# A transformer block on one core: all eight gate pairs by seven block products, a second buffer for the convolution's input, early results stored from ScalarE, the last merged block split by halves

## The chip, the cores and the metric

The kernel runs on one core of a Trainium2 chip, in one launch. The metric is the device time in microseconds (us), and a kernel's time is the median of its runs. Five engines work in parallel, each through its own instructions in a fixed order: TensorE (PE: matmuls, with its weight loads listed as PEld), VectorE (DVE), ScalarE (ACT), GpSimd (POOL) and SyncE (SP). Here SyncE starts most loads, and GpSimd most stores. An engine that waits for another one holds back everything that stands behind the waiting instruction in its own order.

## The reference

One layer of a decoder block on 1024 positions of width 1024. The token mixer takes one modulated, normalised input `h`:

```python
def hybrid_mixer(h, w_in, conv_w, conv_b, conv_ln_g, conv_ln_b, w_conv_out, w_att_out, w_o):
    proj = h @ w_in
    glu_in, qkv, gates = jnp.split(proj, [2 * CONV_WIDTH, 2 * CONV_WIDTH + 3 * ATT_WIDTH], axis=-1)
    u_val, u_gate = jnp.split(glu_in, 2, axis=-1)
    u = u_val * jax.nn.sigmoid(u_gate)
    u = causal_depthwise_conv(u, conv_w, conv_b)
    u = jax.nn.silu(layernorm(u, conv_ln_g, conv_ln_b))
    y_conv = u @ w_conv_out
    qkv = qkv.reshape(b, s, 3, N_HEADS, HEAD_DIM)
    o = stick_breaking_attention(qkv[:, :, 0], qkv[:, :, 1], qkv[:, :, 2])
    y_att = o.reshape(b, s, ATT_WIDTH) @ w_att_out
    g_conv, g_att = jnp.split(gates, 2, axis=-1)
    merged = jax.nn.sigmoid(g_conv) * y_conv + jax.nn.sigmoid(g_att) * y_att
    return merged @ w_o
```

`CONV_WIDTH` and `ATT_WIDTH` are 512, so `gates` is a product of 1024x1024 by 1024x2048. Around the mixer stand norms, a residual, and a feed-forward sub-layer (SwiGLU), which the change doesn't touch.

## The kernel before

Activations lie with channels on the 128 partitions and positions along the free side: `h` is eight tiles of 128x1024, each held as a high part `hhi` and a low part `hlo` (the rest after the high part's rounding). Every product of two matrices is made of three: high by high, high by low and low by high. A weight is loaded raw, ScalarE copies its high part and VectorE subtracts to get the low part (`load_w`, L151 to L159, and `w_op`, L388 to L392). Loads go through SyncE's queue (`load`, L97) and stores through GpSimd's (`store`, L100).

The order of each engine's instructions is not the order of the code. A framework places tiles in pools with a given number of buffers per tag, simulates the program once, and fixes an order for each engine. An edit in one place can therefore move instructions elsewhere.

The mixer's stages around the change, in time:

1. The convolution (`conv`, L438 to L460) of four blocks of channels, as matmuls of 128x128 (L453) of weights `cvw` on a padded copy `ph` of the block. `ph` has one buffer (tag "ph"): it is loaded (L441) from `v_d` in memory, when the block before it has been read to its end. The fourth, `conv(3)`, runs beside attention.
2. Attention, head by head: scores `z` (L543 and L544), transposes `tr` (L566), outputs `av` (L575 and L576). PE works at other products while ScalarE and VectorE work at the scores.
3. The gates. The sixteen blocks of 128 gate channels form eight pairs. A plain pair (the loop over `PLAIN`, L604 to L612) is two products of the whole `h`, two results `pg` of 128x512 per block: 48 matmuls of 128x512 per block, 96 per pair. The other way treats a pair's weights and `h` as 2x2 blocks and makes the four result blocks from seven block products of 12 matmuls each, 84 per pair, with sums of blocks (Winograd's form of Strassen's scheme). With `NPL = 1`, pairs 0 to 6 (`GPAIRS`) take the seven products, and pair 7 is plain.
4. Of the seven, two need only plain blocks of `h`, so they are made early: `early(i, q)` (L615 to L625) loads the raw weight `ew` (q = 0), splits it into `a` (L147 and L391), makes the product `k` (`prod0`, L404, 12 matmuls), evacuates it on ScalarE to `ee` (L624, two buffers of tag "sg"), and stores it through GpSimd (L625): the first product to `e_d0[i]`, the sum of both, after a sigmoid, to `s_d[2 * i]`. Weights `ew` share the three buffers of tag "wraw" with the other raw weights.
5. The other five (`other_five`, L697 to L721) need sums of blocks of `h`, the forms T1 to T4 (L664 to L682). For each j of 0 to 3 four tiles `f` are loaded from `xm_d`, combined on VectorE (L674 to L677), and split into a high part (ScalarE, L147) and a low part (VectorE, L660): `T1o` to `T4o`. The first product of a pair is T2 by `s2o` into the bank `ka`. The weights `gw` of the pair and the early result `ga` are loaded by `pair_load` (L687); VectorE forms the weight sums `gs` (L702 to L707) and the result sums `gv` and `gw` (L710 to L720).
6. The convolution's layer norm (`ln_all`, L737 to L787) with loads `cr` from `u_d`, sums on VectorE (L747, L749, L755) and four small matmuls (L751, L761); then `y_conv` (L795 to L810).
7. Attention's output projection `pya` with the merge (L828 to L844). For each block n of 128 channels the merged `yc` is split into `mhi[n]` and `mlo[n]` as a whole 128x1024 tile (`split_r`, L728: the copy on ScalarE is L147, the subtraction on VectorE L728).
8. The output projection `pwo` (L900) reads `mhi` and `mlo`.

Of the kernel before, what the change touches and what calls it, by code (L numbers as in the profile page):

```python
# [10 lines left out]
F32 = mybir.dt.float32  # L11
F32R = mybir.dt.float32r
AF = mybir.ActivationFunctionType
ALU = mybir.AluOpType
# [3 lines left out]
P = 128  # L18
D = 1024
T = 1024  # L20
KT = D // P
CH = 512
# [6 lines left out]
NG = P // CG  # L29
TM = T // PH  # L30
SH = (TAPS - 2) // PH + 2
# [4 lines left out]
SH_DVE = (5, 6, 7)  # L36
NADA = 5
LATER = 100000
NPL = 1
GORDER = (0, 1, 2, 3, 4, 5, 6, 7)  # L40
NXT = 6
NWT = 4
# [27 lines left out]
def tile_block(ctx: ExitStack, tc: tile.TileContext, xT, vecs, ada1, ada2, win, wv, wcv, wat, wo, w1, w2, cvw, out):  # L70
    nc = tc.nc
    act, dve, pool, pe = nc.scalar, nc.vector, nc.gpsimd, nc.tensor

    def mkpool(stack, name, bufs=1, **kw):
        return stack.enter_context(tc.tile_pool(name=name, bufs=bufs, reuse_waits="tile", **kw))
# [3 lines left out]
    hp = mkpool(ctx, "hp", 16)  # L79
# [6 lines left out]
    s_d = [dp.tile([P, T], F32, name=f"s_d{n}") for n in range(2 * KT)]  # L86
    e_d0 = [dp.tile([P, CH], F32, name=f"e_d0_{i}") for i in range(KT)]
# [9 lines left out]
    def load(dst, src):  # L97
        return nc.sync.dma_start(dst, src)

    def store(dst, src):  # L100
        nc.gpsimd.dma_start(dst, src)
# [43 lines left out]
    def copy_to(eng, dst, src):  # L145
        if eng is act:
            act.activation(dst, src, AF.Copy)  # L147
        else:
            eng.tensor_copy(dst, src)
# [41 lines left out]
    def bank(name):  # L191
        return psm.tile([P, CH], F32, tag="main", name=name)
# [188 lines left out]
    mhi, mlo = [], []  # L381
    HK = KT // 2
    GP = dve
    GPAIRS = GORDER[:KT - NPL]
    PLAIN = [2 * i + q for i in GORDER[KT - NPL:] for q in range(2)]
    B0 = {}

    def w_op(name, src, hi_eng, lo_eng):  # L388
        t = wp.tile([P, 2, CH], F32R, tag=("whi", "wlo")[next(uid) % 2], name=name)
        copy_to(hi_eng, t[:, 0], src)  # L390
        lo_eng.tensor_tensor(t[:, 1], src, t[:, 0], op=ALU.subtract)  # L391
        return t[:, 0], t[:, 1]  # L392

    def prod0(bank_, w, b, first=True):
        for j in range(HK):
            cols = slice(j * P, (j + 1) * P)
            if b[0] == "T":
                mvs = B0[b, j][:, 0], B0[b, j][:, 1]
            else:
                k = j + (HK if b in ("B21", "B22") else 0)  # L400
                cs = slice(CH, T) if b == "B22" else slice(0, CH)
                mvs = hhi[k][:, cs], hlo[k][:, cs]
            for s, (st, mv) in enumerate(((0, 0), (0, 1), (1, 0))):
                pe.matmul(bank_, w[st][:, cols], mvs[mv], start=(first and j == 0 and s == 0),  # L404
                          stop=(j == HK - 1 and s == 2), skip_group_check=not first)

    with ExitStack() as sC:
        pc = mkpool(sC, "pc")
        with ExitStack() as sA:
# [26 lines left out]
                load(channels(v_d[ct]), u)  # L436

            def conv(ct):  # L438
                ph = pc.tile([P, NG, SH - 1 + TM], F32, tag="ph", name=f"ph{ct}", bufs=1)
                pool.memset(ph[:, :, 0:SH - 1], 0.0)  # L440
                load(ph[:, :, SH - 1:], v_d[ct].rearrange("g p m -> p g m"))  # L441
                wts = []
                for hf in range(2):
                    cv = bank(f"pcv{ct}_{hf}")
                    o = sgp.tile([P, NG // 2, TM], F32, tag="sg", name=f"co{ct}_{hf}", bufs=2)
                    for gi in range(NG // 2):
                        g = hf * (NG // 2) + gi
                        for d in range(SH):
                            n, at = divmod((g * SH + d) * P, T)
                            if n == len(wts):  # L450
                                wts.append(wp.tile([P, T], F32, tag="wraw", name=f"cvw{ct}_{n}"))
                                load(wts[n], cvw[ct, n])
                            pe.matmul(cv[:, gi * TM:(gi + 1) * TM], wts[n][:, at:at + P],  # L453
                                      ph[:, g, SH - 1 - d:SH - 1 - d + TM], start=(d == 0), stop=(d == SH - 1))
                    for gi in range(NG // 2):
                        b = C_CB + ct * NG + hf * (NG // 2) + gi
                        act.activation(o[:, gi], cv[:, gi * TM:(gi + 1) * TM], AF.Identity, bias=vec[:, b:b + 1],
                                       scale=1.0)
                    load(u_d[ct][hf * (NG // 2):(hf + 1) * (NG // 2)].rearrange("g p m -> p g m"), o)
# [155 lines left out]
            def early(i, q):  # L615
                if q == 0:
                    raw = wp.tile([P, T], F32, tag="wraw", name=f"ew{i}")
                    load(raw, win[20 + 2 * i])
                    kes[i] = bank(f"k_{i}"), raw
                k, raw = kes[i]  # L620
                w = w_op(f"a1{q + 1}_{i}", raw[:, q * CH:(q + 1) * CH], act, dve)
                prod0(k, w, ("B11", "B21")[q], q == 0)
                e = sgp.tile([P, CH], F32, tag="sg", name=f"ee{q}_{i}", bufs=2)
                act.activation(e, k, (AF.Copy, AF.Sigmoid)[q])  # L624
                store(s_d[2 * i][:, :CH] if q else e_d0[i], e)  # L625

            for n, i in enumerate(GPAIRS):
                early(i, 0)
# [5 lines left out]
    with ExitStack() as sG:  # L634
# [19 lines left out]
        def flat(t):  # L654
            return t.rearrange("p a b -> p (a b)")
# [9 lines left out]
        for j in range(HK):  # L665
            if j == 0:
                f = [pg.tile([P, T], F32, tag="f", name=f"f{q}_{j}", bufs=2) for q in range(2)]
# [57 lines left out]
        def split_r(src, names, hi_eng, lo_eng):  # L725
            hi, lo = (hp.tile([P, T], F32R, tag="act", name=nm) for nm in names)
            copy_to(hi_eng, hi, src)
            lo_eng.tensor_tensor(lo, src, hi, op=ALU.subtract)  # L728
            return hi, lo
# [91 lines left out]
        for p in range(4):  # L821
            of = wp.tile([P, T], F32, tag="wraw", name=f"of{p}")
            load(of, o_d[p])
            hi, lo = (flat(ot(f"{nm}{p}", F32R)) for nm in ("ohi", "olo"))
# [5 lines left out]
        for n in range(KT):  # L830
            if n % 2 == 0:
                wa = load_w(wat[n // 2], f"wa{n}", act, dve)
            sg = [xt(f"sga{n}_{c}") for c in range(NCH)]
            yb = {c: bkg(f"pya{n}_{c}") for c in range(NCH)}
            gemm(yb, wa, (ohi, olo), range(4), woff=(n % 2) * CH)
            y = yc[n]
            for c in range(NCH):
                cs = slice(c * CH, (c + 1) * CH)
                load(sg[c], s_d[8 + n][:, cs])
                last = dve.tensor_tensor(sg[c], yb[c], sg[c], op=ALU.mult)  # L840
                dve.tensor_tensor(y[:, cs], y[:, cs], sg[c], op=ALU.add)
            hi, lo = split_r(y, (f"mhi{n}", f"mlo{n}"), act, dve)
            mhi.append(hi)
            mlo.append(lo)  # L844
        assert not a2
        add_bias(16, 32)
        fold_gate(gpost1, 16, C_POST1)
# [641 lines left out]
    with ExitStack() as sG:  # L1489
# [233 lines left out]
        for m in range(2):  # L1723
            load(ytile["c11", m], c11_d[:, 2 * m:2 * m + 2])
            for i in range(2):
                y = ytile["c11", m][:, i]
                act.activation(y, y, AF.Copy, scale=gpost2[:, 2 * m + i:2 * m + i + 1])
        c21 = out_tiles("c21", (h_tile, h_tile))
        for h in range(2):
# [7 lines left out]
            for n in range(NH):  # L1737
                sq = sq_tile(f"fsq{h}_{n}")[:, :W]
                y = ka[n][:, cols]
                if h == 0:  # L1740
                    y = c21[n][:, cols]
# [74 lines left out]
```

## Time and profile before

The profile is one execution; its own time is a little above the median of the timed runs.

| what | value |
|---|---|
| median of 3 runs | 1413.03 us |
| lowest and highest of them | 1412.89 and 1413.87 us |
| the profiled execution's own time | 1414.92 us |
| its span, first to last instruction | 1413.2 us |
| mean granted clock of PE | 0.99 of full speed |
| busy, share of the span | PE 98%, DVE 74%, ACT 46%, POOL 8% |

Times in the rows of the trace count from the start of the span. A row of the timeline gives start, length (both in us), engine, line, operation, result and operands, how many in a run, and in square brackets the idle time before it with what ended it. A row of the list of waits gives who waited for whom, with the total, the number of times and the longest. "PEclk" in a window is the clock granted to PE, 1.00 for full speed.

### The profile page before, as it was taken

To read this page: it belongs to the slowest core of one execution; us is meant where nothing else is said; L and a number is where in the kernel's file an instruction comes from. 1 tells how busy PE (TensorE), PEld (TensorE's weight loads), DVE (VectorE), ACT (ScalarE), POOL (GpSimd) and SP (SyncE) were. 2 spreads that over 40 slices of the span, in tenths; PEclk is the share of its full clock that TensorE was granted. 3 is DMA by queue.
4 is the path that set the end of the run, shared out by engine and by line. 5 is a ranking of instruction groups with operands and counts; after the bars stand their busy time and mean duration, and the time that the engine had idled before them with its cause. 6 is when DMAs were issued, how large, how long until landed. Compare 5 with 4: busy or idle time off the path is not lost.

```text
span 1413.2 us, 18854 instructions
## 1 busy us (share of the span) xinstructions
PE 1378.3 (98%) x6810; PEld 1157.3 (82%) x6810; DVE 1048.3 (74%) x1591; ACT 655.3 (46%) x1146; POOL 117.4 (8%) x262
## 2 busy tenths in 40 slices
PE   7999999999998999999999999999999999999996
PEld 5898898998886788788877778888888887888886
DVE  7897687675865888878589878778877776785355
ACT  6375566364554455512356553334434443434441
POOL 0100001000001111000011110001111110000002
PEclk8999999999999999999999999999999999999998
DMA  9512051140348554973934545456777769586736
GB/s 382 200 39 82 16 164 30 46 150 30 120 150 298 208 170 148 349 226 124 360 120 163 182 148 177 165 171 212 260 250 246 264 240 387 177 337 221 254 116 120
DMA packets 93789, 265.02 MB, mean 188 GB/s; under 512 B 10048, under 2 KB 21440, under 8 KB 92672
## 3 DMA queue, kind: packets, MB, share of 16 engines
q1 hardware_dynamic: 74352, 201.68, 42.0%
q0 software_dynamic: 19344, 62.14, 12.4%
q8 instruction: 53, 0.87, 0.3%
q14 instruction: 40, 0.33, 0.1%
HBM read 192.74 MB, written 71.04 MB: 187 GB/s over the span
## 4 chain that ended last, share of the span: by engine, by line
PE 75%; issue 9%; DVE 8%; DMA 4%; ACT 2%; POOL 1%; SPq 0%; DVEq 0%; POOLq 0%; ACTq 0%
PE ka L982 14%; PE ka L1524 9%; PE kc L982 8%; PE pwo L900 6%; PE pb L1524 4%; PE pgv L168 3%; PE pv L473 3%; PE pgg L168 2%; PE pk L168 2%; PE pq L168 2%; PE ke L1090 2%; PE pcv L453 2%; PE tr L566 2%; PE pa L1524 2%; PE kb L982 2%
## 5 line engine op out<-in xcount | busy, mean ns | idle before, releaser
L545 ACT ACTIVATE ka<-z 128x128 f32<-128x128 f32 (+2 forms) x96 | 47.0, 496 | 55.8 <-PE z L544 51.9
L551 DVE TENSOR_TENSOR_SCAN ka<-ka,eye 128x128 f32<-128x128 f32 (+1 forms) x64 | 52.1, 831 | 23.2 <-ACT ka L545 23.0
L570 DVE TENSOR_TENSOR alo<-tr,ahi 128x512 fp32r<-128x512 f32 x80 | 53.4, 685 | 21.3 <-ACT ahi L569 20.7
L569 ACT ACTIVATE ahi<-tr 128x512 fp32r<-128x512 f32 x80 | 46.7, 603 | 39.1 <-PE av L575 22.9
L1524 PE MATMUL ka<-gt,w2f 128*128 128x512 f32 x264 | 63.4, 389 | 0.0
L556 DVE TENSOR_TENSOR be<-be,ka 128x127 f32<-128x127 f32 (+2 forms) x96 | 51.2, 550 | 12.1 <-ACT be L547 8.5
L1524 PEld LDWEIGHTS ka<-gt,w2f 128*128 128x128 f32 x264 | 49.5, 188 | 10.3
L123 DVE SCALAR_TENSOR_TENSOR ada<-ada,cb 128x1024 f32<-128x1024 f32 x32 | 38.9, 1223 | 23.6 <-DMA ada<-in_ada_dram 23.4
L1090 PE MATMUL ke<-b,w_hi 128*128 128x512 f32 x176 | 55.2, 395 | 0.0
L547 ACT ACTIVATE be<-z 128x127 f32<-128x127 f32 (+2 forms) x96 | 46.4, 496 | 17.8 <-PE tr L566 17.6
L566 PE MATMUL tr<-ident,be 128*128 128x128 f32 x288 | 46.6, 272 | 0.0
L453 PE MATMUL pcv<-ph,cvw 128*128 128x128 f32 x320 | 43.7, 282 | 2.5 <-DMA ph<-v_d 2.5
L554 DVE TENSOR_TENSOR_SCAN ka<-ka 128x512 f32<-128x512 f32 x32 | 40.4, 1274 | 6.3 <-ACT ka L545 6.3
L404 PE MATMUL k<-hhi,a 128*128 128x512 f32 x112 | 38.3, 413 | 6.6 <-ACT ee L624 6.6
L453 PEld LDWEIGHTS pcv<-ph,cvw 128*128 128x128 f32 x320 | 41.5, 198 | 3.5 <-issue 2.7
L575 PE MATMUL av<-ahi,vst 128*128 128x256 f32 x160 | 43.8, 291 | 0.0
L576 PE MATMUL av<-alo,vst 128*128 128x256 f32 x160 | 42.2, 290 | 0.0
L1090 PEld LDWEIGHTS ke<-b,w_hi 128*128 128x128 f32 x176 | 32.9, 188 | 7.9 <-issue 1.0
L147 ACT ACTIVATE gt<-X 128x512 fp32r<-128x512 f32 x33 | 20.3, 629 | 39.4 <-DVE X L1567 14.3
L473 PE MATMUL pv<-wv_hi,hhi 128*128 128x256 f32 x128 | 36.7, 287 | 1.6 <-DVE vst L478 0.9
L147 ACT ACTIVATE s1o<-s 128x512 fp32r<-128x512 f32 x22 | 13.8, 629 | 48.8 <-PE ka L982 41.0
L473 PE MATMUL pv<-wv_lo,hhi 128*128 128x256 f32 x128 | 36.3, 285 | 0.0
(545 smaller groups left out, 4145.8 us busy)
## 6 DMA issues: line engine op xcount, KB each, us to landing
w_d<-w2o POOLq DMA_DIRECT2D x44, 512.0 KB, 7.6
w2f<-w_d SPq DMA_DIRECT2D x44, 512.0 KB, 4.5
ada<-in_ada_dram SPq DMA_DIRECT2D x32, 512.0 KB, 5.7
w2r<-in_w_dram SPq DMA_DIRECT2D x44, 256.0 KB, 3.8
w1g<-in_w_dram SPq DMA_DIRECT2D x21, 512.0 KB, 3.7
w1u<-in_w_dram SPq DMA_DIRECT2D x21, 512.0 KB, 5.7
cvw<-in_cvw_dram SPq DMA_DIRECT2D x20, 512.0 KB, 3.8
ada_w<-in_ada_dram SPq DMA_DIRECT2D x8, 1024.0 KB, 13.9
```

The costliest lines, as they stand in the source:

```text
L168: pe.matmul(bank, st[:, cols], mv[k][:, c * CH:(c + 1) * CH], start=(i == 0 and s == 0), stop=(i == n - 1 and s == 2))
L453: pe.matmul(cv[:, gi * TM:(gi + 1) * TM], wts[n][:, at:at + P], ph[:, g, SH - 1 - d:SH - 1 - d + TM], start=(d == 0), stop=(d == SH - 1))
L473: pe.matmul(pv[:, :256], st[k][:, tcols], mv[:, wc], start=(k == 0 and i == 0), stop=(k == KT - 1 and i == 2))
L545: act.activation(kap[:, s_lo:s_hi], z[:, zo:zo + w], AF.Sigmoid, bias=0.0, scale=-0.125)
L551: dve.tensor_tensor_scan(rev, rev, eye[:, CH - w:][:, ::-1], 0.0, op0=ALU.mult, op1=ALU.add)
L556: dve.tensor_tensor(beta[:, :m], beta[:, :m], kap[:, s_lo + 1:s_lo + 1 + m], op=ALU.mult)
L566: pe.transpose(tr[:, o:o + P], src, ident)
L570: dve.tensor_tensor(alo, tr, ahi, op=ALU.subtract)
L900: pe.matmul(bank_, st[:, cols], mv[k][:, cs], start=(k == 0 and q == 0), stop=(k == KT - 1 and q == 2))
L982: pe.matmul(bank_, st[:, cols], t[:, mv], start=(first and j == 0 and s == 0), stop=(j == HK - 1 and s == 2), skip_group_check=not first)
L1090: pe.matmul(kbs[f], wes[f][st][:, cols], t[:, mv], start=(i == 0 and j == 0 and q == 0), stop=(j == HK - 1 and q == 2), skip_group_check=i ...
L1524: pe.matmul(dst, w[st][:, cols], g[mv], start=first and s == 0, stop=last and s == 2, skip_group_check=more)
```

## The change

Four edits:

- `NPL` goes from 1 to 0: pair 7, too, is made by seven products; `PLAIN` is empty.
- `ph` has two buffers instead of one.
- The sixteen early results are started by ScalarE instead of GpSimd.
- The last merged block (n = 7) is split into its parts by halves of 512 columns, each right after its sum; the other seven are split whole, as before.

```diff
--- before.py
+++ after.py
@@ -36,7 +36,7 @@
 SH_DVE = (5, 6, 7)
 NADA = 5
 LATER = 100000
-NPL = 1
+NPL = 0
 GORDER = (0, 1, 2, 3, 4, 5, 6, 7)
 NXT = 6
 NWT = 4
@@ -436,7 +436,7 @@
                 load(channels(v_d[ct]), u)
 
             def conv(ct):
-                ph = pc.tile([P, NG, SH - 1 + TM], F32, tag="ph", name=f"ph{ct}", bufs=1)
+                ph = pc.tile([P, NG, SH - 1 + TM], F32, tag="ph", name=f"ph{ct}", bufs=2)
                 pool.memset(ph[:, :, 0:SH - 1], 0.0)
                 load(ph[:, :, SH - 1:], v_d[ct].rearrange("g p m -> p g m"))
                 wts = []
@@ -622,7 +622,7 @@
                 prod0(k, w, ("B11", "B21")[q], q == 0)
                 e = sgp.tile([P, CH], F32, tag="sg", name=f"ee{q}_{i}", bufs=2)
                 act.activation(e, k, (AF.Copy, AF.Sigmoid)[q])
-                store(s_d[2 * i][:, :CH] if q else e_d0[i], e)
+                act.dma_start(s_d[2 * i][:, :CH] if q else e_d0[i], e)
 
             for n, i in enumerate(GPAIRS):
                 early(i, 0)
@@ -839,9 +839,17 @@
                 load(sg[c], s_d[8 + n][:, cs])
                 last = dve.tensor_tensor(sg[c], yb[c], sg[c], op=ALU.mult)
                 dve.tensor_tensor(y[:, cs], y[:, cs], sg[c], op=ALU.add)
-            hi, lo = split_r(y, (f"mhi{n}", f"mlo{n}"), act, dve)
-            mhi.append(hi)
-            mlo.append(lo)
+                if n < KT - 1:
+                    continue
+                if c == 0:
+                    mhi.append(hp.tile([P, T], F32R, tag="act", name=f"mhi{n}"))
+                    mlo.append(hp.tile([P, T], F32R, tag="act", name=f"mlo{n}"))
+                act.activation(mhi[n][:, cs], y[:, cs], AF.Copy)
+                dve.tensor_tensor(mlo[n][:, cs], y[:, cs], mhi[n][:, cs], op=ALU.subtract)
+            if n < KT - 1:
+                hi, lo = split_r(y, (f"mhi{n}", f"mlo{n}"), act, dve)
+                mhi.append(hi)
+                mlo.append(lo)
         assert not a2
         add_bias(16, 32)
         fold_gate(gpost1, 16, C_POST1)
```

The order of every engine's instructions changes from `conv(3)` on, and is the same again from the output projection on. Three places follow.

On PE, around the start of `conv(3)` (`tr`, `z` and `av` belong to attention; `pcv_0_4111` is the first half of `conv(3)`), as one piece of the difference, after (+) against before (-):

```order
 L566 MATMUL tr_0_0_0_3844<-ident,zeros 128x128
 L566 MATMUL tr_0_0_0_3844<-ident,be_0_1_0_3835 128x128
+L453 MATMUL pcv_0_4111<-ph_4108,cvw_0_4113 128x128
 L543 MATMUL z_1_6_0_3907<-kst_1_3035,qst_1_3033 128x512
 L544 MATMUL z_1_6_0_3907<-klo_1_3037,qst_1_3033 128x512
+L453 MATMUL pcv_0_4111<-ph_4108,cvw_0_4113 128x128
 L543 MATMUL z_1_7_0_3915<-kst_1_3035,qst_1_3033 128x512
 L544 MATMUL z_1_7_0_3915<-klo_1_3037,qst_1_3033 128x512
...
 L543 MATMUL z_1_4_1_3950<-kst_1_3035,qst_1_3033 128x256
 L544 MATMUL z_1_4_1_3950<-klo_1_3037,qst_1_3033 128x256
-L453 MATMUL pcv_0_4111<-ph_4108,cvw_0_4113 128x128 x8
```

Two of the first eight matmuls are seen to move up, and six more (four and two) stand in the rows left out; all eight are now among attention's products ahead of `z_1_4_1`, where before they came behind it.

On SyncE, at the end of attention, before (`o_d` is attention's output, `f` the tiles of the forms, `ada` weights of a later stage, `ew` an early weight, `gw0a` and `gw0b` the weights of pair 0):

```order
L98 DMA o_d_69<-oT_3610 128x1024
L98 DMA ew_4476<-in_win_dram 128x1024
L98 DMA f_0_4585<-xm_d_103 128x512 x2
...
L98 DMA f_3_4656<-xm_d_106 128x512
L98 DMA ew_4515<-in_win_dram 128x1024
L98 DMA gw0a<-in_win_dram 128x1024
L98 DMA ada_16_5535<-in_ada_dram 128x1024
L98 DMA ada_17_5538<-in_ada_dram 128x1024
L98 DMA gw0b<-in_win_dram 128x1024
L98 DMA f_3_4657<-xm_d_110 128x512
L98 DMA f_3_4658<-xm_d_110 128x512
```

And now (`cr` are the layer norm's loads):

```order
L98 DMA gw0b<-in_win_dram 128x1024
L98 DMA o_d_69<-oT_3610 128x1024
L98 DMA gw1a<-in_win_dram 128x1024
L98 DMA f_0_4500<-xm_d_103 128x512 x2
...
L98 DMA f_3_4571<-xm_d_106 128x512
L98 DMA cr_4909<-u_d_74 128x1024
...
L98 DMA cr_4912<-u_d_77 128x1024
L98 DMA ada_16_5553<-in_ada_dram 128x1024
L98 DMA ada_17_5556<-in_ada_dram 128x1024
L98 DMA f_3_4572<-xm_d_110 128x512
L98 DMA f_3_4573<-xm_d_110 128x512
```

The weights of pair 0 and the first of pair 1 now stand ahead of the first tile `f`, and four loads `cr` with two of `ada` ahead of the last two tiles `f_3`. Row `gw1a` waits for VectorE's `a_7_4469`, the low part of the last early weight, to free its buffer.

On VectorE, from the first form to the last part of T2 (the row `T2o` that reads `f_3`), before, where 39 operations stand from the one to the other:

```order
L674 TENSOR_TENSOR f_0_4585<-f_0_4585 128x512
...
L391 TENSOR_TENSOR a_6_4554<-ew_4515,a_6_4554 128x512
...
L660 TENSOR_TENSOR T4o_4652<-f_2_4634,T4o_4652 128x512
L702 TENSOR_TENSOR gs_0_4691<-gw0b 128x512
L675 SCALAR_TENSOR_TENSOR f_3_4655<-f_3_4657,dsh_4583,f_3_4655 128x512
L703 TENSOR_TENSOR gs_0_4692<-gs_0_4691,gw0a 128x512
...
L676 SCALAR_TENSOR_TENSOR f_3_4657<-f_3_4657,mod,f_3_4656 128x512
...
L677 SCALAR_TENSOR_TENSOR f_3_4658<-f_3_4658,mod,f_3_4657 128x512
L707 TENSOR_TENSOR gs_0_4692<-gw0a,gs_0_4692 128x512
L660 TENSOR_TENSOR T2o_4667<-f_3_4657,T2o_4667 128x512
```

And now, where there are 45:

```order
L391 TENSOR_TENSOR a_7_4469<-ew_4430,a_7_4469 128x512
L674 TENSOR_TENSOR f_0_4500<-f_0_4500 128x512
...
L660 TENSOR_TENSOR T2o_4558<-f_2_4548,T2o_4558 128x512
L747 TENSOR_TENSOR la<-cr_4909,cr_4910 128x512
...
L391 TENSOR_TENSOR a_0_4685<-gw0b,a_0_4685 128x512
L707 TENSOR_TENSOR gs_0_4607<-gw0a,gs_0_4607 128x512
L675 SCALAR_TENSOR_TENSOR f_3_4570<-f_3_4572,dsh_4498,f_3_4570 128x512
...
L677 SCALAR_TENSOR_TENSOR f_3_4573<-f_3_4573,mod,f_3_4572 128x512
L755 TENSOR_TENSOR cr_4909<-cr_4909,lm 128x512
...
L755 TENSOR_TENSOR cr_4912<-cr_4912,lm 128x512
L660 TENSOR_TENSOR T2o_4582<-f_3_4572,T2o_4582 128x512
```

The splits of early weights no longer stand between the forms, since all sixteen now come ahead of the first one; seven operations of the layer norm (L747, L749, L755) and the rest of pair 0's weight sums have moved ahead of the last part of T2. On PE, 82 early matmuls now stand between attention's last product and the first product with T2, where 124 stood; and where pair 7's 96 plain matmuls and 8 early ones stood beside the last attention head, there are now 110 early ones. From there to the output projection follow 462 matmuls after the last part of T2 can start, against 456 before from T2's start.

## The prediction

> **What bounds the kernel now.** The page of the profile comes first. Its busy line says that TensorE (PE) has work nearly all the time, so the time changes through PE's work, PE's gaps and PE's clock.
>
> ```profile
> PE 1378.3 (98%) x6810; PEld 1157.3 (82%) x6810; DVE 1048.3 (74%) x1591; ACT 655.3 (46%) x1146; POOL 117.4 (8%) x262
> ```
>
> Next the list of waits of PE, which names every stall (total, times, longest). Four kinds touch edited code or its neighbours.
>
> ```profile
> PE k L404 <- ACT ee L624: 6.6, 4, 4.0
> PE pcv L453 <- DMA ph<-v_d: 2.5, 1, 2.5
> PE pwo L900 <- ACT mhi L147: 1.3, 1, 1.3
> PE ka L404 <- DVE gv L710: 0.9, 1, 0.9
> ```
>
> To place them, the windows of 10 us around those stalls (after the bounds: length, then busy us of PE, PEld, DVE, ACT, POOL, then the granted clock, DMA share, GB/s).
>
> ```profile
> 380.00:390.00 10.00, 7.46 (x50) 7.24 (x49) 6.06 (x9) 3.62 (x9) 0.00 (x0) 0.83 0.53 158
> 390.00:400.00 10.00, 10.00 (x83) 9.74 (x82) 7.39 (x11) 7.55 (x17) 0.20 (x2) 1.00 0.67 204
> 430.00:440.00 10.00, 10.00 (x47) 8.31 (x46) 3.03 (x5) 3.67 (x7) 1.55 (x3) 1.00 0.87 288
> 440.00:450.00 10.00, 8.25 (x36) 6.17 (x34) 7.17 (x12) 5.50 (x10) 1.08 (x2) 1.00 1.05 411
> 450.00:460.00 10.00, 6.04 (x24) 4.35 (x24) 10.00 (x17) 5.67 (x12) 1.08 (x2) 1.00 1.00 382
> 460.00:470.00 10.00, 9.07 (x28) 7.25 (x29) 10.00 (x17) 6.27 (x12) 2.15 (x4) 0.66 0.49 174
> ```
>
> PE is full from 390 to 440; it has holes at 380 to 390 (the convolution's load) and from 440 to 470, where the early products (k) wait for ScalarE's evacuation ee. In that second hole VectorE is busy in every microsecond from 450 to 470: it makes the forms T1 to T4 that the big products need. That is the row to remember: removing the named wait (ee) does not help if PE then waits for the forms.
>
> **The change part by part**
>
> *Seven products for pair 7 as well.* A plain pair is 96 matmuls of 128x512, seven products are 24 early and 60 late ones, 84. One costs what a run without stalls shows, in the chain of waits:
>
> ```profile
> 460.93 8.45 PE k L404 x24
> 472.10 5.44 PE k L404 x24
> ```
>
> The lower row is 5.44/24 = 0.227 us each. The work falls by 12 x 0.227 = 2.7 us. (The upper row, right after the longest stall, is the same 24 at a lowered clock: 3.0 us more.) But the 96 plain matmuls stood between 400 and 430, where they filled PE beside the last attention head. By the order, 110 early matmuls now fill it instead of 96 plain and 8 early (+6, 1.4 us there). So after the last attention product only 82 early ones are left before the big products, where there were 124.
>
> *Second buffer of ph.* The stall, in PE's timeline, and the load that ends it, in the chain:
>
> ```profile
> 376.12 2.84 PE L453 MATMUL pcv<-ph,cvw 128*128 128x128 f32 x24
> 384.49 4.32 PE L453 MATMUL pcv<-ph,cvw 128*128 128x128 f32 x22 [2.54 <-DMA ph<-v_d]
> ```
> ```profile
> 379.03 5.33 DMA ph<-v_d
> ```
> ```profile
> 366.13 0.33 SPq L98 DMA_DIRECT2D v_d<-u  x1
> ```
>
> Before the gap 24 matmuls take 2.84 us; after it 22 take 4.32, where 22 x 2.84/24 = 2.60 is full speed. So the gap costs 2.54 + 1.72 = 4.3 us. With a second buffer the load no longer waits for the old convolution; it needs only v_d, written from 366.13 on. Even with the 5.33 us of the store's and again of the load's way it is there by about 377 to 379, when the new order first wants it. I take the whole 4.3. Ends: 2.5 (the clock dips for another gap) and 4.3, or 0 if a weight load comes late in its stead.
>
> [...]
>
> So the last attention product comes 4.3 - 1.4 = 2.9 us earlier. Here it stands at 430.41, and the first big product at 469.22, 38.5 us after its end:
>
> ```profile
> 430.41 0.28 PE L576 MATMUL av<-alo,vst 128*128 128x256 f32 x1
> 460.93 0.80 PE L404 MATMUL k<-hhi,a 128*128 128x512 f32 x1 [4.01 <-ACT ee L624]
> 469.22 2.88 PE L404 MATMUL ka<-T2o,s2o 128*128 128x512 f32 x12
> ```
>
> *The stretch after attention.* The forms set it now. First the loads (SyncE's queue) and the forms (VectorE):
>
> ```profile
> 432.07 0.33 SPq L98 DMA_DIRECT2D o_d<-oT  x1
> 433.41 11.90 SPq L98 DMA_DIRECT2D f<-xm_d  x14
> 454.82 1.53 SPq L98 DMA_DIRECT2D f<-xm_d  x2
> ```
> ```profile
> 441.15 0.69 DVE L674 TENSOR_TENSOR f<-f 128x512 f32<-128x512 f32 x1 [0.72 <-DMA f<-xm_d]
> 444.71 0.69 DVE L391 TENSOR_TENSOR a<-ew,a 128x512 fp32r<-128x512 f32 x1 [1.64 <-ACT a L147]
> 459.65 0.69 DVE L660 TENSOR_TENSOR T2o<-f,T2o 128x512 fp32r<-128x512 f32 x1
> 460.25 0.68 DVE L660 TENSOR_TENSOR T1o<-f,T1o 128x512 fp32r<-128x512 f32 x1
> 462.66 0.75 DVE L675 SCALAR_TENSOR_TENSOR f<-f,dsh,f 128x512 f32<-128x512 f32 x1
> 463.32 0.69 DVE L703 TENSOR_TENSOR gs<-gs,gw0a 128x512 f32<-128x512 f32 x1
> 467.06 0.69 DVE L660 TENSOR_TENSOR T2o<-f,T2o 128x512 fp32r<-128x512 f32 x1
> ```
>
> The last T2 form was ready at 467.75, 1.5 us before PE took it up: PE was late by that much, and everything that could be gained in the early products alone (edit 3 among it) is 1.5 us. In the new order the loads f stand behind gw1a on SyncE, and gw1a waits for the lo half of the last early weight. That half needs the buffer of the early product whose last 10 matmuls follow attention (10 x 0.227 = 2.3 us), then a ScalarE copy and a VectorE subtraction, each behind its engine's other work: about 4.8 us after attention against 2.7 here (433.41 - 430.7). The first form follows the first load by 5 to 7.7 us here (441.15 - 433.41), so it starts at 10 to 12.5. From it to the last T2 form VectorE's order holds 45 operations, where it held 39; 0.60 us each (460.25 - 459.65) or 0.66 (463.32 - 462.66) gives about 28 us, since 7 operations of the layer norm and more of the scale sums now stand ahead of it. So T2's last part is ready at 38.5 (10 + 28 + an eviction of slack) after attention: the interval that it has today. Ends: 35 (loads as early as today, nothing in between) and 42.5 (first form at 12.5, and 2 us of gaps).
>
> PE meanwhile has 82 early matmuls and 19 others, 101 x 0.227 = 23 us, in those 38.5, so about 15 us of idling, where it idled 6.6 and lost 3.0 to the clock. The ee waits vanish into this idling; their cover is the wait for forms. PE then restarts at a lowered clock as it did at 460.93: 3.0 us at most, I take 2.7, low end 0, if the 19 matmuls come just before. What remains after that point is 462 matmuls against 456: +1.4. One of the layer-norm products falls into the idle time, -0.6 (590 ns each, by the groups of instructions):
>
> ```profile
> L751 PE MATMUL lnm<-la,ones 128*128 128x512 f32 x4 | 2.0, 590 | 0.0
> ```
>
> The 0.9 us for gv goes in part, since VectorE is ahead: -0.4 (ends -0.9 and +1).
>
> *Early results on ScalarE's queue.* Now and then:
>
> ```profile
> 442.51 0.60 ACT L624 ACTIVATE ee<-k 128x512 f32<-128x512 f32 x1 [2.80 <-DMA e_d<-ee]
> ```
> ```profile
> 443.40 0.54 POOL L101 DMA_DIRECT2D s_d<-ee  x1 [6.53 <-ACT ee L624]
> ```
> ```profile
> 436.32 7.15 DMA e_d<-ee
> ```
>
> GpSimd starts its issue 0.3 us after the evacuation's end (443.11) and spends 0.54; that is what can be saved of each store, beside a transfer of 7.15. The issue now stands in ScalarE's own order, ahead of form copies. Priced at 0, covered by the wait for forms; ends -1.5 (above) and +1 (16 issues at SyncE's 0.33 are 5.3 us, of which ScalarE's gaps take most).
>
> *Last merged block by halves.*
>
> ```profile
> 670.87 1.06 ACT L147 ACTIVATE mhi<-yc 128x1024 fp32r<-128x1024 f32 x1 [3.88 <-DVE yc L841]
> ```
> ```profile
> 671.97 0.73 PE L900 MATMUL pwo<-mhi,wo_hi 128*128 128x512 f32 x2 [1.27 <-ACT mhi L147]
> ```
>
> The first half's copy no longer waits for VectorE's second half (0.6) and is itself half as long, so the 1.27 goes nearly whole: -1.2 (ends 0 and -1.5, with the two matmuls more that now precede).
>
> **Sum**, on the profiled run of 1414.92: attention's end -2.9; forms at the same distance 0; lowered clock +2.7; six more matmuls behind +1.4; layer norm -0.6; gv -0.4; merged block -1.2; together -1.0. The profiled run lies 1.9 above the median of 1413.03, so the forecast is 1413.03 - 1.0 = 1412.0, no change that a measurement can tell. [...] The count of 2.7 us less work is nearly all given back as idling.
>
> **The rivals**
>
> 1. *Faster: forms early, clock kept.* VectorE is free of a's splits once the early weights are done, so forms may run straight at 35 instead of 38.5 (-3.5), and the scattered matmuls may keep the clock (-2.7): 1405.8. For it: VectorE was busy for only 7.17 us from 440 to 450, with forms under way, because a split of an early weight held them up (the row at 444.71, after 1.64 us of waiting). Against: seven more operations ahead of T2, and the later loads.
>
> 2. *Slower: the last loads f.* The last two (f_3) now stand behind four cr and two ada loads. They came 9.5 us after the end of the 14 (454.82 - 445.31) today; from an end at 16.7 (4.8 + 11.9) that gives 26, and up to 30 if each cr waits for a free lane; landing takes about 7 (the median of these loads, in the row below), and eight VectorE operations with a ScalarE copy follow before T2 (5 to 6 us): 38 to 44. It decides above 41. At 44: +5.5, 1417.5. Against: today's 9.5 already hold five other loads.
>
> ```profile
> f<-xm_d SPq DMA_DIRECT2D x16, 256.0 KB, 6.8
> ```
>
> 3. *ph is waited for all the same* (the change does not do what it says): v_d's store or a convolution weight is late, and 2 to 4 us stay: 1414 to 1416.
>
> 4. *The early results do decide:* if ScalarE's issues delay the form copies, T2 comes 1 to 2 us later, 1413 to 1414; inside "same".
>
> **How the numbers follow.** Forecast with rival 4 and half of rival 3: 0.42. Rival 1 or a good part of it: 0.33. Rival 2: 0.18. The worse half of rival 3 with other small losses: 0.07. What a measurement of this kernel can tell from no change is about 0.2%, 2.8 us, so the bounds are 1410.2 and 1415.9. The forecast's own spread of some 3 us puts a little over each: faster 0.36, same 0.40, slower 0.24. The range of 8 in 10 runs from rival 1 (1405.8, a little lower with T2 at 34.5) to rival 2: 1405 to 1418. The forecast alone: 1409 to 1415.
>
> **What would show it.** Right: no wait on ph, the window there full at clock 1.00; last attention product at about 427.5; after it no long ee wait that matters, but waits of T2's products on VectorE's T2o of 12 to 18 us in sum, first full T2 product ending near 467 to 469; pwo's wait gone. Wrong: forms ready by 35 us after attention (rival 1), f_3's landing named as the wait (rival 2), or PE's holes between 390 and 430, which would mean that early weights come too slowly to fill the last attention head; I have priced that at nothing, since a load there serves 24 matmuls and a copy with a subtraction 12, and VectorE and ScalarE have gaps there (the windows at 390 and 430).

## The result and the profile after

The changed kernel takes 1418.72 us (median of 15 runs, 1416.68 to 1424.6) against 1413.03 before (15 runs): the ratio is 1.0042, 95% interval 1.003 to 1.0055, so 4 to 8 us slower. The forecast was 1412.0, no change, within 1405 to 1418.

The profiled execution after took 1416.92 us. TensorE's (PE's) list of waits, for the stretch from 440 to 672 us:

```profile
PE kc L404 <- ACT s1o L147: 9.8, 1, 9.8
PE ka L404 <- ACT s2o L147: 2.7, 2, 2.1
PE ka L404 <- DVE T2o L660: 2.0, 1, 2.0
PE kc L404 <- DVE T1o L660: 0.5, 1, 0.5
```

The waits on `ph` and on `ee` are gone. In their place stand 15.0 us of waits of T1 and T2 products of pair 0 and, for the 2.1, of pair 1. The windows (length, then busy us of PE, PEld, DVE, ACT, POOL, clock, DMA share, GB/s) show the same:

```profile
380.00:390.00 10.00, 10.00 (x83) 9.73 (x83) 8.56 (x14) 7.10 (x20) 0.20 (x2) 1.00 0.72 206
440.00:450.00 10.00, 6.93 (x30) 5.07 (x28) 9.84 (x16) 5.83 (x11) 0.00 (x0) 0.94 1.04 386
450.00:460.00 10.00, 2.67 (x6) 1.66 (x7) 10.00 (x17) 5.29 (x10) 0.00 (x0) 0.50 1.02 406
460.00:470.00 10.00, 7.49 (x22) 4.46 (x20) 9.96 (x17) 5.50 (x10) 0.00 (x0) 0.84 0.33 113
470.00:480.00 10.00, 7.90 (x26) 6.36 (x27) 8.24 (x14) 3.14 (x5) 0.38 (x1) 0.69 0.27 78
```

The window of the convolution is full at clock 1.00. After attention PE idles through most of 450 to 460, and the clock is still down at 470 to 480, where before it was full again:

```profile
470.00:480.00 10.00, 10.00 (x46) 8.29 (x45) 6.04 (x10) 2.92 (x6) 1.08 (x2) 1.00 0.76 269
```

PE's timeline after the change gives the steps:

```profile
427.74 0.28 PE L576 MATMUL av<-alo,vst 128*128 128x256 f32 x1
456.74 1.22 PE L404 MATMUL kc<-T1o,s1o 128*128 128x512 f32 x2 [9.81 <-ACT s1o L147]
467.83 0.73 PE L404 MATMUL ka<-T2o,s2o 128*128 128x512 f32 x2 [2.03 <-DVE T2o L660]
472.10 1.22 PE L404 MATMUL ka<-T2o,s2o 128*128 128x512 f32 x2 [2.11 <-ACT s2o L147]
473.97 3.96 PE L404 MATMUL ka<-T3o,s3o 128*128 128x512 f32 x12
```

Attention's last product ends at 428.02, 2.7 us earlier than before (430.69). T2's last part is taken up at 467.83. But pair 0's next product, T3, starts only at 473.97. VectorE's timeline shows why; `gv` is the sum that reads the bank `ka` before T3 adds to it:

```profile
438.99 0.69 DVE L674 TENSOR_TENSOR f<-f 128x512 f32<-128x512 f32 x1 [6.81 <-DMA f<-xm_d]
464.68 2.49 DVE L755 TENSOR_TENSOR cr<-cr,lm 128x512 f32<-128x512 f32 x4
467.09 0.68 DVE L660 TENSOR_TENSOR T2o<-f,T2o 128x512 fp32r<-128x512 f32 x1
470.10 0.68 DVE L759 TENSOR_TENSOR la<-la,lm 128x512 f32<-128x512 f32 x1
472.02 0.69 DVE L710 TENSOR_TENSOR gv<-ka,ga 128x512 f32<-128x512 f32 x1
```

And the same row before:

```profile
472.14 0.69 DVE L710 TENSOR_TENSOR gv<-ka,ga 128x512 f32<-128x512 f32 x1 [0.68 <-PE ka L404]
```

Before, `gv` waited for PE. Now it waits for nothing but VectorE itself, which from the second form to here is never idle for more than a tenth of a microsecond, the layer norm's operations (L747 to L759) among them. PE waits for VectorE in turn: by then it has started 108 matmuls since attention's last product, where before the change it had started 137.

Single executions differ by some us in their first 60 us already (last section), so profiles are compared here from the store of attention's first half of heads on (`o_d`, at 343 to 348 us). From there to the end of the last attention product the two profiles of before take 87.07 and 86.46 us, four of the change 84.01 and three times 84.00. From that product to the first of the output projection: before 233.73 and 233.53, the change 239.44, 241.24, 239.82 and 241.23. From there to the end: 748.78 and 746.56, against 747.74, 748.30, 747.74 and 748.06. In the mean: 2.8 us won, 6.8 lost, and 0.3 lost, together 4.3 us, at the low end of the interval above.

### The profile page after: what moved, and what is told of

The parts are those of the page before. It is cut to its first block, busy times and chain, and to the rows that moved or that the text cites. A ratio compares the mean times of both kernels' runs of the same rounds, so it can differ in the third digit from the quotient of the medians.

```text
span 1415.2 us, 18858 instructions
## 1 busy us (share of the span) xinstructions
PE 1376.1 (97%) x6798; PEld 1154.6 (82%) x6798; DVE 1054.8 (75%) x1606; ACT 659.1 (47%) x1153; POOL 109.0 (8%) x247
## 4 chain that ended last, share of the span: by engine, by line
PE 84%; DVE 7%; DMA 4%; issue 2%; ACT 2%; SPq 0%; DVEq 0%; ACTq 0%
PE ka L990 14%; PE ka L1532 9%; PE kc L990 8%; PE pwo L908 6%; PE ka L404 5%; PE pb L1532 4%; PE pgv L168 3%; PE kc L404 3%; PE pv L473 3%; PE k L404 3%; PE tr L566 2%; PE pgg L168 2%; PE pq L168 2%; PE pk L168 2%; PE pcv L453 2%
## 5 line engine op out<-in xcount | busy, mean ns | idle before, releaser
L404 PE MATMUL kc<-T1o,s1o 128*128 128x512 f32 x96 | 28.4, 423 | 10.3 <-ACT s1o L147 9.8
```

## The experiments

Each kernel was timed against the kernel before on the same chip. Differences are the ratio times 1412.5 us, with its 95% interval.

**The first edit alone (npl0)**

```diff
-NPL = 1
+NPL = 0
```

> Only the first edit: all eight pairs by seven products, the other three edits undone. Theory A (lost cover: the 96 plain matmuls were what kept TensorE busy while VectorE makes the forms, and the idling that follows also lowers the granted clock): the loss of the whole change, 5.7 us, plus what the second ph buffer (4.3) and the halves (0.8) brought, so 1423 to 1424 us, with about 15 us of waits of the first T1 and T2 products on VectorE or ScalarE. Theory B (ScalarE's order: the stores that it starts hold back the copies of the forms): 1409 to 1413 us, since the stores are GpSimd's here. The recorded forecast's sum would give 1417.

Measured: 1426.09 us against 1412.57, +12.7 (9.2 to 16.4). Theory A said 1423 to 1424, 2 to 3 us less but inside the interval; theory B said at most 1413, and falls. The first edit is the one that costs, more than the other three give.

**All but the first edit (all_but_npl0)**

```diff
-NPL = 0
+NPL = 1
```

> The change without its first edit: pair 7 plain again, the second ph buffer, the stores on ScalarE and the halves kept. Theory A: the cover is back, so before less ph (4.3) and the halves (0.8), and the early stores at most 1.5: 1406 to 1409 us, no wait on ph, ee waits of 4 to 7 us as before. Theory B: the ScalarE stores still cost, so 1413 to 1418 us.

Measured: 1409.49 us, -3.7 (-5.7 to -1.7), half a microsecond above theory A's range and below theory B's. The other three edits make the kernel faster. In the order for this kernel 122 early matmuls stand between attention and T2, and the ee waits are back (5.2 us in three).

**Filling the longest wait (filler)**

```diff
             early(GPAIRS[-1], 1)
+            for m in range(4):
+                dm = bank(f"dm{m}")
+                for j in range(12):
+                    pe.matmul(dm, hhi[j % KT][:, 0:P], hhi[(j + m) % KT][:, 0:CH], start=(j == 0), stop=(j == 11))
```

> The whole change with 48 matmuls of 128x512 added whose result nobody reads, put by the order among and behind the last early products (48 x 0.227 = 10.9 us, about the longest wait of 9.8). Theory D (a part of the loss is the lowered clock after the idling, and its length differs from run to run): the wait of 9.8 is filled, the clock is full at the first T1 product, and the time is 1414 to 1416 us, with runs closer together (within 3 us of each other, against 8). If the idling itself is all of the loss: 1418 to 1420 us and the same spread.

Measured: 1422.93 us, +10.6 (7.5 to 13.7), a miss for both readings. PE's timeline of this kernel:

```profile
469.08 0.50 PE L404 MATMUL ka<-T2o,s2o 128*128 128x512 f32 x1 [1.46 <-ACT T2o L147]
472.70 1.22 PE L404 MATMUL ka<-T2o,s2o 128*128 128x512 f32 x2 [2.60 <-DVE T2o L664]
475.77 1.22 PE L404 MATMUL ka<-T2o,s2o 128*128 128x512 f32 x2 [0.99 <-ACT s2o L147]
```

The wait of 9.8 us is filled and the clock is full from 440 to 470, yet PE comes to the same waits for T2's last part and pair 1's sum, and the clock falls there (0.55 from 470 to 480). Here a full clock ahead of the wait for VectorE gained nothing. Why this order is slower than the change itself isn't settled; some of the added matmuls stand ahead of the last early products, and a later wait of 2.3 us (565 us) has no counterpart in the change's profile.

**The layer norm held back (norm_later)**

```diff
-                dve.tensor_tensor(s0_, cr[0][:, cs], cr[1][:, cs], op=ALU.add)
+                with tc.issue_after(formed[-1].ins):
+                    dve.tensor_tensor(s0_, cr[0][:, cs], cr[1][:, cs], op=ALU.add)
```

(`formed` collects VectorE's low halves of the forms, the last one being T4's fourth part.)

> The whole change with the layer norm's first sum on VectorE held back until the last form is done, so that its seven operations (some 4.3 us) no longer stand ahead of T2's last part; all else keeps its order there. Theory C (VectorE's order ahead of T2 sets the time): T2's last part is ready about 4 us sooner, 35 to 36 us after the last attention product, and the time falls to 1414 to 1416 us. If the wait is set by something else (a load, ScalarE's copies): 1418 to 1419 us.

Measured: 1412.47 us, -0.7 (-2.8 to 1.3) against before, so 6 to 7 less than the change, more than was expected. The rows of its profile, whose last attention product ends at 432.40:

```profile
467.44 0.69 DVE L660 TENSOR_TENSOR T2o<-f,T2o 128x512 fp32r<-128x512 f32 x1
469.36 0.69 DVE L711 TENSOR_TENSOR gv<-ka,ga 128x512 f32<-128x512 f32 x1
```
```profile
461.00 1.22 PE L404 MATMUL kc<-T1o,s1o 128*128 128x512 f32 x2 [9.55 <-ACT s1o L147]
470.10 3.01 PE L404 MATMUL ka<-T3o,s3o 128*128 128x512 f32 x12 [0.59 <-DVE gv L711]
```

T2's last part is ready 35.7 us after attention (in the change 39.8), `gv` at 37.7 (44.7), and T3 starts at 37.7 (46.0). The longest wait, 9.55, is still there. From attention's last product to the output projection this profile takes 236.39 us, 4.0 less than the change's mean of 240.43, so a part of what T3 gains is lost again behind it, and the medians' 6 to 7 us are more than this one profile shows. Holding one operation back also moved others: `gv` now comes third behind T2's last part, and pair 1's first products come behind T3. So this run shows what VectorE's order is worth as a whole, not the layer norm's seven operations alone.

**Pair 1 behind pair 0's T3 (pair1_behind)**

```diff
+            if i == 1:
+                with tc.issue_after(third[0].ins):
+                    prod0(ka, s2o, "T2")
```

(and the same for T1; `third` holds pair 0's last matmul with T3.)

> The whole change with one thing altered in TensorE's order: pair 1's products with T2 and T1 are held behind pair 0's product with T3 (four matmuls of pair 1 stood ahead of it and waited 2.1 to 2.3 us for ScalarE's copy of pair 1's sum); VectorE's and ScalarE's orders stay as they are, the layer norm's seven operations ahead of T2 too. If that order is what the layer norm acts through: pair 0's T3 starts at about 42 us after the last attention product instead of 46, 1414 to 1416 us. If the layer norm's delay of T2 itself is the loss: 1418 to 1420, unchanged.

Measured: 1420.04 us, +7.2 (4.9 to 9.6), unchanged. The four matmuls of pair 1 no longer stand in front, and T3 waits all the same, by its own reader:

```profile
473.42 5.49 PE L404 MATMUL ka<-T3o,s3o 128*128 128x512 f32 x12 [2.51 <-DVE gv L717]
```
```profile
472.67 0.69 DVE L717 TENSOR_TENSOR gv<-ka,ga 128x512 f32<-128x512 f32 x1
```

So the order of PE is not by itself what costs. T3 needs `gv`, and `gv` stands where VectorE comes to it.

**The change again, three times (change_again, change_third, change_fourth)**

> The changed kernel again, unaltered, beside the others on one chip. If the loss is in the stretch between the last attention product and the output projection, a second profile shows the same two or three waits there (T1 and T2 on ScalarE's and VectorE's copies, 14 to 20 us) while the time at which attention begins may differ by some us from execution to execution, as the clock at the start of the kernel does. 1416 to 1420 us.

> The changed kernel again, unaltered, for a third profile. Its 22 executions so far lie between 1416.7 and 1425.3 us; the two profiled ones were 1416.9 and 1419.6. If the length differs by where the clock is lowered, a slow execution shows the same waits after attention and more matmuls at the lowered clock; if by a wait that comes and goes, a wait that the two others don't have.

> The changed kernel once more, unaltered, for a fourth profile, with the same two readings as the third: either more matmuls at the lowered clock after the same waits, or a wait that the shorter executions do not show.

Measured: 1419.2 us in seven runs, +7.6 (4.7 to 10.6), and single executions of 1417.51 and 1423.26. All show the same waits after attention, so neither reading holds there. The longest execution differs ahead of the change: `o_d` is stored at 348.21 in it, at 344.01 to 344.26 in the other three, and the rest takes 1073.3 us against 1071.2 to 1073.5. Their windows from 30 to 60 us, of the third and then the fourth:

```profile
30.00:60.00 30.00, 29.62 (x143) 24.64 (x142) 29.20 (x43) 8.96 (x11) 5.19 (x15) 0.97 0.71 292
```
```profile
30.00:60.00 30.00, 30.00 (x125) 25.28 (x124) 29.29 (x43) 8.91 (x11) 5.27 (x15) 0.80 0.71 291
```

**Two plain pairs (two_plain)**

```diff
-NPL = 1
+NPL = 2
```

> The kernel before with NPL at 2 instead of 1: pairs 6 and 7 plain, so 12 matmuls more (2.7 us) and 220 instead of 124 matmuls between the last attention product and the first T2. Theory A (TensorE is short of cover there): the waits on ee and their lowered clock, 9.6 us in the profile before, go, and the kernel gains 9.6 - 2.7 = 6.9: 1405 to 1407 us although it computes more. If the seven products' saving of matmuls is what counts: 1415 to 1416 us.

Measured: 1414.75 us, +2.4 (0.6 to 4.4), not the 1405 to 1407 of theory A, and near the other reading's 1415, but for another reason. The stretch after attention is as theory A had it:

```profile
440.00:450.00 10.00, 10.00 (x45) 8.27 (x45) 10.00 (x17) 6.27 (x13) 0.47 (x1) 1.00 0.95 372
450.00:460.00 10.00, 10.00 (x46) 8.26 (x45) 9.56 (x16) 6.30 (x13) 2.15 (x4) 1.00 0.73 242
460.00:470.00 10.00, 10.00 (x46) 8.29 (x45) 4.48 (x8) 4.72 (x9) 2.16 (x4) 1.00 0.85 276
```

No wait, full clock. What it wins is lost at the output projection:

```profile
PE pwo L900 <- DVE sga L840: 6.7, 1, 6.7
```

The result banks of the gate pairs, and of the products behind them, are dealt out in a fixed pattern. With two results fewer the pattern shifts, and the projection's first bank is one that the last merged block still reads.

**The same with the second and fourth edit (two_plain_ph_halves)**

```diff
-NPL = 1
+NPL = 2
...
-                ph = pc.tile([P, NG, SH - 1 + TM], F32, tag="ph", name=f"ph{ct}", bufs=1)
+                ph = pc.tile([P, NG, SH - 1 + TM], F32, tag="ph", name=f"ph{ct}", bufs=2)
```

(and the halves as in the change.)

> The same with the second ph buffer and the halves of the last merged block (the early stores stay on GpSimd). The parts add if they are independent: 6.9 + 4.3 + 0.8 less than before, 1400 to 1402 us. If the ph stall's gain is taken back by a later wait: 1404 to 1406.

Measured: 1410.95 us, -1.1 (-3.2 to 0.8), above both readings. With the projection's wait (6.5 us) in place, the parts measured alone (+2.4 for two plain pairs, -4.5 for the second buffer, below) add up to -2.1, inside the interval.

**Two plain pairs with the banks dealt anew (two_plain_ph_halves_banks)**

```diff
-        uidg = count()
+        uidg = count(2)
...
-            if next(uidg) % 7 in (1, 4, 6):
+            u = next(uidg)
+            if u == 3 or u % 7 in (1, 4, 6):
```

> Pairs 6 and 7 plain, the second ph buffer and the halves, and the result banks of the gate pairs dealt out so that the output projection's first bank is not the one that the last merged block reads (two more numbers in the count that deals them, and one more bank from the shared pool). In the run without this the projection waited 6.5 us for that block and ran at a lowered clock afterwards (some 2 us). Without the wait: 1403 to 1405 us, the fastest so far. If the wait is for something else (the merge's loads or sums): 1410 to 1412, unchanged.

Measured: 1405.63 us, -8.2 (-10.5 to -5.9), the fastest kernel here, with 12 matmuls more than the kernel before and 24 more than the change. The wait of 6.5 us is gone but for 0.2; the longest wait of the projection is another and shorter:

```profile
PE pwo L909 <- ACT mhi L848: 1.7, 1, 1.7
```

**The second edit alone, and with the fourth (ph_alone, ph_halves)**

> The second edit alone, the second ph buffer. By the recorded sum 4.3 us less than before (2.54 of waiting and 1.72 of lowered clock). [...]

> The change without its first and third edits: the second ph buffer and the halves alone. By the terms (4.3 and 0.8): 1407 to 1409 us. Against the run with the stores on ScalarE as well (1409.5) this gives the third edit's own price: equal within 1 us if it is nothing, as the forecast had it; 1 to 3 us lower here if ScalarE's issues delay its copies.

Measured: 1408.49 us, -4.5 (-6.5 to -2.5), and 1408.76, -3.7 (-5.7 to -1.7). The second buffer agrees with its term of 4.3 us; in its profile the stretch from `o_d` to attention's end is 83.05 us, 3.4 to 4.0 less than in the two of before. The halves add nothing that can be measured, and the stores on ScalarE (1409.49 with them, above) neither.

**All but the third edit (all_but_act_store)**

```diff
-                act.dma_start(s_d[2 * i][:, :CH] if q else e_d0[i], e)
+                store(s_d[2 * i][:, :CH] if q else e_d0[i], e)
```

> The change without its third edit: the early stores start on GpSimd again. The recorded sum prices the edit at nothing, with ends of -1.5 and +1: 1417 to 1420 us against the 1419 of the whole change. Theory B (ScalarE's order pays for the stores) would give 1413 to 1416; a store that lands sooner and frees ee sooner would give over 1421.

Measured: 1422.07 us, +8.8 (6.2 to 11.4), against +5.9 (4.2 to 7.8) for the change: the intervals overlap, so the medians cannot tell the edit from nothing. A cost of ScalarE's issues does not show: without them the kernel is 2.9 slower here, and in the other pair (ph_halves and all_but_npl0) both are at -3.7. The median lies in the range of the third reading, over 1421, but not for its reason, since the waits on `ee` come to 0.2 us in the whole stretch. The order is another, and PE's waits on ScalarE's copies `s2o` come to 8.2 us, where the change's four profiles have 2.7 to 3.7.

This run also settles what T3 waits for, since here T2's last part comes early and the layer norm's four L755 stand behind it:

```profile
465.72 0.62 PE L404 MATMUL ka<-T2o,s2o 128*128 128x512 f32 x2
473.21 4.58 PE L404 MATMUL ka<-T3o,s3o 128*128 128x512 f32 x12
```
```profile
464.52 0.69 DVE L660 TENSOR_TENSOR T2o<-f,T2o 128x512 fp32r<-128x512 f32 x1
467.53 2.49 DVE L755 TENSOR_TENSOR cr<-cr,lm 128x512 f32<-128x512 f32 x4
471.25 0.69 DVE L710 TENSOR_TENSOR gv<-ka,ga 128x512 f32<-128x512 f32 x1
```

Attention's last product ends at 427.77. T2's last part is ready 37.4 us after it, 2.3 sooner than in the change, and PE takes it up without a wait. But `gv` is done at 44.2 (44.7) and T3 starts at 45.4 (46.0): it follows `gv`, not T2's last part.

**The kernel before again (before_again)**

> The kernel before, unaltered, for a second profile. In the first one both stalls of this stretch (2.5 us on ph, 4.0 us on ee) were followed by a lowered clock, which my sum took as certain (1.7 and 3.0 us). Theory E: a stall of that length lowers the clock in some executions only, so this profile shows at least one of them without it, and from the store of attention's first output to the end it is 2 to 5 us shorter than the 1069.6 us of the first profile. If the loss always follows: 1069 to 1070 again.

Measured: 1411.62 us in eight runs. Theory E falls for the two stalls, though the time is 3 us shorter as it had it: both are followed by a lowered clock again. Behind the 4.00 us on `ee` the clock is 0.66 from 460 to 470, and the 24 early matmuls take 8.3 us up to the next product, where the next 24 take 5.4. The convolution's, in this second profile of before:

```profile
385.00 4.32 PE L453 MATMUL pcv<-ph,cvw 128*128 128x128 f32 x22 [1.90 <-DMA ph<-v_d]
```

Its time from `o_d` on is 1066.6 us, 3 less than in the first profile. 0.6 of that lies before the last attention product; 2.2 lie behind the start of the output projection, where no edit changes the order.

## Why the prediction was wrong, point by point

**Right: the end of attention.** The last product was forecast at about 427.5 (430.41 - 2.9); it starts at 427.74. The second buffer alone measures -4.5 us, the term was 4.3. The wait alone, 2.5 us, the low end of the term, is the edge of the measured interval, and the two profiles of before speak against it: behind a wait of 2.54 and one of 1.90 us the next 22 matmuls took 4.32 us, where 2.60 is full speed.

**Near: the idling and the forms.** PE idles 12.4 us between attention and T2's end (9.81, 0.58 and 2.03); the text had about 15. T2's last part is ready 39.8 us after attention; the text had 38.5 with ends of 35 and 42.5. The sign was not met by name: only 2.0 us are put down to T2o, and the 9.8 are a wait for `s1o`, the copy of pair 0's weight sum L702, which stands at 455.35 in VectorE's order among the forms. The lowered clock at the restart was priced at 2.7. From 467.83 to T3's end at 477.93 PE does 20 matmuls, 4.5 us at full clock (0.227 us each); of the 10.1 us it waits 2.6 (0.47 and 2.11), so 3.0 go to the clock.

**Wrong: the step "PE then restarts".** The sum took T2's last part as the last thing that PE needs from VectorE, and let PE run free behind it ("What remains after that point is 462 matmuls against 456: +1.4"). It is not the last thing. Pair 0's T3 adds to the bank that `gv` must read first, and `gv` comes eight places behind T2's last part in VectorE's new order, with L759 and three of pair 1's sums (L702, L703, L705) ahead of it. In the old order it came seven places behind T2's last part, and VectorE was there before PE; the 24 early products between T2 and the next product (the row of 5.44 us in the prediction) covered it. In the change there are none left. T3 starts 46.0 us after attention and 6.1 behind the start of T2's last part on PE (473.97 - 467.83), with eight matmuls in between (1.8 us at full clock); of that the sum had only the clock. In the change's own profile the wait of 2.11 in these 6.1 us carries another name, pair 1's `s2o`, since four matmuls of pair 1 stand ahead of T3; pair1_behind takes them away, and T3 then waits 2.51 for `gv` and starts 45.1 us after attention.

The loss of this stretch was expected at 2.7 + 1.4 - 0.6 - 0.4 = 3.1 and measured at 6.8 in the mean of the profiles. Most of the 3.7 more are the 1.3 to 1.8 by which PE takes up T2's last part later than forecast (39.8 to 40.3 in the four profiles, against 38.5) and the 2.2 to 2.8 of waits between that and T3. Shown by all_but_act_store, where T2's last part is 2.3 us sooner and T3 still follows `gv`; by pair1_behind, where PE's order is changed and the time is not; and by norm_later, where `gv` comes 7 us earlier and the kernel is faster, by 6 to 7 us in the medians and 4.0 in its profile. (The 462 and 456 count the block products alone. In the traces PE does 850 matmuls of all kinds from T2's last part to the output projection, and before 848 from T2's start: two more, 0.5 us, where the sum had 1.4 - 0.6.)

**Wrong: "VectorE is ahead".** The 0.9 us for `gv`, from which the sum took 0.4, stand at 569.10 us in the profile before, at a later pair, and are gone. At pair 0 VectorE had been ahead because PE had early products left, and that is what the edit took away. The operations were counted up to T2, 45 of them; up to `gv` there are 53 from the first form, 33.7 us, and PE's early products cover only the first 8 of these (to 446.93).

**Wrong: the merged block.** -1.2 was expected. ph_halves against ph_alone shows nothing, and the time from the projection's first matmul to the end is the same in the mean. The wait on the last block was shortened (0.5 us after, 1.0 in change_again, none in two profiles), but not to be seen in the time; before_again doesn't show the 1.3 us at all.

**The rivals.** Rival 2 came nearest in time (1417.5), but its sign did not come: from 440.09 to `gv` VectorE waits for no load. Its number is near by luck. Rival 1 did not come either, since T2's last part was ready at 39.8 and not at 35; in norm_later, with the layer norm out of the way, it is ready at 35.7.

**The third edit** was priced at nothing, and the medians cannot tell it from nothing. But it changes the order: with pair 7 by seven products the stretch from attention to the projection is 244.42 us without it against 239.44 to 241.24 with it, and with pair 7 plain 233.28 against 234.88, from one profile each but for the change's four.

**The size.** The price of the first edit is the 9.6 us between the change (+5.9) and all_but_npl0 (-3.7); change_again gives 11.3. The saving of 12 matmuls is real, and all of it and more is given back because the early products were the only work that PE had while VectorE made the forms. Two plain pairs show the reverse: 2.7 us more work, and no wait in that stretch.

npl0 fits this: +5.9 for the change, 4.5 for the missing second buffer and 2.9 for the stores give 13.3 if each is taken at its median, and 12.7 was measured. Its waits on `s2o` come to 7.9 us, where all_but_act_store has 8.2.

What stays open: why the difference of the medians (4 to 8 us) is centred some 2 us above that of the profiled executions, why norm_later gains more in the medians than in its profile, and why filler is slower than the change.

## What to carry to other kernels

A saving of matmuls counted here only where TensorE had other work ready: 12 less, 2.7 us of work, made this kernel 9.6 us slower. Count what is left as cover in the stretch where another engine sets the pace, and if it runs out, follow that engine's order to the last operation that TensorE's next products need, banks that must be read before they are added to included, not to the first. When a scheduler moves ready work (here a layer norm) ahead of the operations that TensorE waits for, holding it back can win back a good part of what an edit cost (here 4 to 7 us). A pattern that deals out banks belongs to the count of results: when the count changes, look at who takes over the last bank (here a wait of 6.7 us in two_plain).

## What the runs showed of the hardware that was not expected

A short stall lowered the clock here in some places, and its length alone did not decide. Behind waits of 1.90 and 2.54 us on the convolution's load the next 22 matmuls took 4.32 us; behind one of 1.67 us (two_plain) the same 22 took 2.69, which is nearly full speed (2.60):

```profile
384.71 2.69 PE L453 MATMUL pcv<-ph,cvw 128*128 128x128 f32 x22 [1.67 <-DMA ph<-v_d]
```

At a later pair's T2 product a wait of 2.16 us (all_but_act_store, at 563 us) left the clock full, the 12 matmuls with T3 behind it taking 2.91, while behind one of 2.58 us (npl0, at 565 us) the 12 with T3 took 5.32, at a granted clock of 0.71 from 560 to 570.

In the first 60 us, which no edit touches, single executions come out at a granted clock of 0.80 to 0.82 or of 0.93 to 0.97 in the window from 30 to 60 us (the changed kernel at 0.80 once and at 0.93 to 0.97 three times), and everything behind is about 4 us later in the first case (348.21 against 344.1 in the change's four profiles). A difference between two profiles of a few us should be taken from a point behind that.
